# Rewriting the junctures between the branches of an eight-branch transformer kernel: pairs through PSUM, a pinned VectorE order, a shorter root, later transposes

## The chip, the cores and the metric

The program runs on one core of one Trainium2 chip. The metric is the device time of one execution in microseconds (us); of several runs the median counts. The engines are TensorE (PE in the rows, its weight loads PEld), VectorE (DVE), ScalarE (ACT), GpSimd (POOL) and SyncE (SP), which issues the DMAs. SBUF is the working memory, PSUM the memory that TensorE writes to.

## What is computed

Eight branches follow each other on one residual stream x of 512 tokens and 1024 features: two attention blocks, and then twice an FFN, a token mixer and an FFN. Every branch begins with a norm and ends with a norm and an addition:

```python
# attention block            # FFN and mixer of the second part
h = rms_norm(x, pre_norm)    h = swiglu(rms_norm_2(x, g[0]), w_in, w_out)
y = mix(h @ w_in) @ w_out    x = x + 0.5 * rms_norm_2(h, g[1])
x = x + rms_norm(y, post)    h = token_mixer(rms_norm_2(x, g[2]), ...); x = x + rms_norm_2(h, g[3])

def rms_norm(x, g):
    return x * lax.rsqrt(jnp.mean(x * x, axis=-1, keepdims=True) + 1e-6) * g
```

All is float32. Where one branch ends and the next begins lies a juncture: the post norm of y, the addition to x, and the pre norm of the new x. There are seven of them between branches, and the end of the last branch is half of one.

## The kernel before

**Layout.** Activations are transposed: features on the 128 partitions in eight chunks, tokens in the columns, handled in two halves of 256 (`HALF`). `XT` holds x, `Y` (tag `big`) the output of a branch, `xh` and `xl` the normed input of the next branch, split into a high part in a TensorE format (float32r) and the rest. Each product is three matmuls (`mm3`, L238 to L243): high by high, high by low, low by high. Weights are split the same way, high part by ScalarE (L282), rest by GpSimd or VectorE (L283).

**Scales are put off.** The gain is multiplied into xh and xl at once, the reciprocal root of the mean square is not: products are taken of the unscaled x, and their results are multiplied by the row `R` when they leave PSUM. So a norm needs the sum of squares (`square`: ScalarE squares, GpSimd adds, L345), then the sum over partitions by a matmul with ones (`ss_matmul`, L331), the root on VectorE (`rsqrt` and `newton`, L245 to L263: a bit trick and three Newton steps), and two transposes by TensorE that spread it over the partitions (`col_bcast`, L298), copied out of PSUM by ScalarE (L380) into `P` (post norm) or `R` (pre norm).

**The juncture** (`juncture`, L399 to L417) goes, for each half, over eight chunks: VectorE multiplies y by P (L409, or L411 where the gain is still to be multiplied in, which is so behind an FFN), adds it to x (L413), ScalarE makes xh (L372), VectorE xl (L373), ScalarE squares x and GpSimd adds the square. Behind the last branch the sum goes to the output instead, and GpSimd takes eleven of the sixteen additions. P of the first half is made (`post_done`) in the middle of the last products of the old branch.

**The lead** (`lead`, L435 to L468) is the first work of each branch: two weight units of 256 columns by eight chunks, for half 0 with both units chunk by chunk, for half 1 first unit 0 and then unit 1. `pre_cols` (sum and root) and `pre_rows` (transposes and copy) stand between its products, as do the evacuations. A unit and half take two PSUM tiles of 256 columns, one for each 128 output features.

**Order.** The framework's planner orders the instructions of each engine by the order in which they are traced, by when its cost model has their inputs ready, and by `high_priority`, which the root and the copies of its row have. Each engine works through its own queue in order. PSUM has eight banks: four `sc`, two `mm`, two `tp`. Squares and their sums take their buffers from the pool of the lead's weights.

**Names that the prediction uses.** L839 and L115 are VectorE instructions of the attention heads that read one tensor from PSUM and one from SBUF. L1161 are transposes in the mixer's gate chain, whose input is a running sum on VectorE (L1143 to L1146) of the gate product `pg`, evacuated at L1132.

Of the kernel before, what the change touches and what calls it, by code (L numbers as in the profile page):

```python
# [23 lines left out]
F32 = mybir.dt.float32  # L24
# [7 lines left out]
S = 512  # L32
HALF = (slice(0, 256), slice(256, 512))
ALL = slice(0, 512)
D = 1024
# [10 lines left out]
MAGIC = float(0x5F3759DF)  # L46
# [157 lines left out]

class Kern:
    def __init__(self, ctx, tc, ap):
# [4 lines left out]
        self.wp = Pool(ctx.enter_context(tc.tile_pool(name="wp", bufs=3)))  # L211
        self.rp = Pool(ctx.enter_context(tc.tile_pool(name="rp", bufs=2)))
# [5 lines left out]
        self.leads = 0  # L218

# [18 lines left out]
    def mm3(self, out, lhs, rhs, start, stop):  # L238

        nc = self.nc  # L240
        nc.tensor.matmul(out, lhs[0], rhs[0], start=start, stop=False)  # L241
        nc.tensor.matmul(out, lhs[0], rhs[1], start=False, stop=False)  # L242
        nc.tensor.matmul(out, lhs[1], rhs[0], start=False, stop=stop)  # L243

    def rsqrt(self, src, n, mul, add, name, y=None):  # L245

        v = self.nc.vector
        x = self.sm(n, name + "x")
        v.tensor_scalar(x, src, mul, add, op0=OP.mult, op1=OP.add)
        return self.newton(x, n, name, y)  # L250

    def newton(self, x, n, name, y=None):

        v = self.nc.vector
        y = self.sm(n, name + "y") if y is None else y
        t = self.sm(n, name + "t")
        v.tensor_scalar(t.bitcast(I32), x.bitcast(I32), 1, None, op0=OP.logical_shift_right)
        v.tensor_scalar(y.bitcast(I32), t.bitcast(I32), -1.0, MAGIC, op0=OP.mult, op1=OP.add)
        for _ in range(3):
            v.tensor_tensor(t, y, y, op=OP.mult)  # L260
            v.scalar_tensor_tensor(t, t, -0.5, x, op0=OP.mult, op1=OP.mult)
            v.scalar_tensor_tensor(y, t, 1.5, y, op0=OP.add, op1=OP.mult)
        return y  # L263
# [63 lines left out]
    def ss_matmul(self, q, n):  # L327

        p = self.tp()
        for tb in range(n):  # L330
            self.nc.tensor.matmul(p[:, 0, tb:tb + 1], q[:, tb * 128:(tb + 1) * 128], self.ones[:, 0:1],  # L331
                                  start=True, stop=True)
        return p[:, 0, :n]
# [14 lines left out]

    def rms(self, st, y=None):

        x0, x = self.sm(2, "x0"), self.sm(2, "rnx")
        s0 = self.ss_matmul(st["acc"], 2)
        s1 = self.ss_matmul(st["last"], 2) if "last" in st else None
        with self.tc.high_priority():
            if s1 is None:
                return self.rsqrt(s0, 2, 1.0 / D, EPS, "rn", y)
            self.nc.vector.tensor_scalar(x0, s0, 1.0 / D, EPS, op0=OP.mult, op1=OP.add)
            self.nc.vector.scalar_tensor_tensor(x, s1, 1.0 / D, x0, op0=OP.mult, op1=OP.add)
            return self.newton(x, 2, "rn", y)
# [16 lines left out]
    def rows(self, r, out):  # L376

        p = self.col_bcast(r, 2).rearrange("p a b -> p (a b)")
        with self.tc.high_priority():
            self.nc.scalar.copy(out, p[:, 0:256])  # L380

    def pre_cols(self, t):
        self.rms(self.pre[t], self.r[:, 2 * t:2 * t + 2])

    def pre_rows(self, t):
        self.rows(self.r[:, 2 * t:2 * t + 2], self.R[:, HALF[t]])

    def post_done(self, st, t):
        if t == 0:
            self.P = self.lead_pool.tile([128, S], F32, name="P", tag="P", bufs=1)  # L390
        self.rows(self.rms(st), self.P[:, HALF[t]])

    def prenorm(self, g):
        self.next_in()
        for t in range(2):
            for c in range(KC):
                self.pre_chunk(self.pre[t], c, g, HALF[t])

    def juncture(self, Y, gpost, nxt):  # L399


        nc = self.nc
        if nxt:
            self.next_in()
        for t, sl in enumerate(HALF):
            for c in range(KC):
                y, x, P = Y[:, c, sl], self.XT[:, c, sl], self.P[:, sl]
                if gpost is None:
                    nc.vector.tensor_tensor(y, y, P, op=OP.mult)  # L409
                else:  # L410
                    nc.vector.scalar_tensor_tensor(y, y, gpost[:, c:c + 1], P, op0=OP.mult, op1=OP.mult)  # L411
# [23 lines left out]
    def lead(self, evac):  # L435
# [5 lines left out]
        def run(us, t, ks):  # L441
# [1022 lines left out]
```

## Time and profile before

| | us |
|---|---|
| median of three runs | 2952.69 |
| the runs | 2944.2, 2952.69, 2952.72 |
| the profiled execution | 2944.85 |
| its span, first to last instruction | 2942.0 |
| mean granted TensorE clock | 0.977 |

The profile's times are those of one execution, from the start of its span. A row of the timeline merges like instructions that follow each other (x4). "Idle before" is the time that an engine stood still ahead of a group, with what ended it. [...]

### The profile page before, as it was taken

What the parts mean: (1) busy time and instruction counts of PE and PEld (TensorE: products, weight loads), DVE (VectorE), ACT (ScalarE), POOL (GpSimd) and SP (SyncE); (2) the same over time, 40 slices, a digit from 0 to 9 for tenths busy, and PEclk for the clock granted to TensorE, in tenths of its full rate; (3) what the DMA queues carried; (4) which work ended last, traced back from release to release, by engine and by line L of the source; (5) the groups of instructions that cost most, each with busy time, mean ns of one, the idle gap of its engine ahead of it and who ended that gap; (6) DMA issues with size and microseconds to landing.
All of it is one profiled execution on the core that took longest, in us unless ns stands there. A gap on an engine that the chain in (4) does not pass through costs nothing.

```text
span 2942.0 us, 43303 instructions
## 1 busy us (share of the span) xinstructions
PE 2778.2 (94%) x16048; PEld 2427.3 (83%) x16048; DVE 1513.0 (51%) x3398; ACT 1381.3 (47%) x2937; POOL 1347.9 (46%) x1265
## 2 busy tenths in 40 slices
PE   7999999998999988899899998999998899899997
PEld 7997899877888887798888888888887798888886
DVE  6489757987303257857730225312246857731132
ACT  6578547874333334657433334323333648432332
POOL 4553445434444544333444545444453433534545
PEclk9999999999999999999999999999999999999999
DMA  4111211121232212111222322223221220223332
GB/s 170 58 44 51 80 48 44 44 83 62 95 99 97 92 52 80 58 65 60 96 96 88 106 90 69 93 87 108 84 84 48 76 73 30 87 73 94 101 96 74
DMA packets 69283, 230.54 MB, mean 78 GB/s; under 512 B 8968, under 2 KB 11912, under 8 KB 68816
## 3 DMA queue, kind: packets, MB, share of 16 engines
q1 hardware_dynamic: 69072, 227.78, 23.8%
q8 instruction: 126, 2.06, 0.3%
q14 instruction: 85, 0.70, 0.1%
HBM read 225.51 MB, written 2.24 MB: 77 GB/s over the span
## 4 chain that ended last, share of the span: by engine, by line
PE 69%; DVE 20%; ACT 5%; issue 2%; POOL 1%; DMA 1%; DVEq 0%; POOLq 0%; SPq 0%; ACTq 0%
PE sc L242 11%; PE sc L243 11%; PE sc L241 10%; PE mm L241 10%; PE mm L243 10%; PE mm L242 10%; DVE XT L413 2%; DVE xl L373 2%; PE sc L110 1%; PE tp L139 1%; DVE big L411 1%; DVE nm L186 1%; DVE O L1183 1%; DVE E L198 1%; DVE pl L143 1%
## 5 line engine op out<-in xcount | busy, mean ns | idle before, releaser
L283 POOL TENSOR_TENSOR wl<-wr,wh 128x512 fp32r<-128x512 f32 x732 | 943.5, 1299 | 943.1 <-ACT wh L282 905.0
L282 ACT CAST wh<-wr 128x512 fp32r<-128x512 f32 x836 | 502.8, 614 | 733.3 <-PE sc L242 476.7
L242 PE MATMUL sc<-xl,wh 128*128 128x512 f32 (+1 forms) x1600 | 602.9, 377 | 4.3 <-DVE xl L373 4.1
L243 PE MATMUL sc<-xh,wl 128*128 128x512 f32 (+1 forms) x1600 | 601.9, 376 | 0.3 <-DVE wl L283 0.2
L241 PE MATMUL sc<-xh,wh 128*128 128x512 f32 (+1 forms) x1600 | 600.1, 376 | 2.3 <-ACT xh L372 2.2
L484 DVE TENSOR_TENSOR fg<-sc,R 128x512 f32<-128x512 f32 (+1 forms) x88 | 58.7, 667 | 758.8 <-PE sc L243 756.3
L242 PEld LDWEIGHTS sc<-xl,wh 128*128 128x128 f32 x1600 | 307.1, 192 | 59.1 <-DVE xl L373 6.5
L241 PEld LDWEIGHTS sc<-xh,wh 128*128 128x128 f32 x1600 | 305.7, 192 | 55.8 <-ACT xh L372 3.3
L243 PEld LDWEIGHTS sc<-xh,wl 128*128 128x128 f32 x1600 | 307.4, 192 | 53.1 <-DVE wl L283 0.7
L345 POOL TENSOR_TENSOR sacc<-sacc,sq 128x256 f32<-128x256 f32 x222 | 190.3, 864 | 247.3 <-ACT sq L343 223.8
L241 PE MATMUL mm<-wh,xh 128*128 128x256 f32 x1024 | 295.7, 289 | 0.3 <-DVE G L854 0.3
L243 PE MATMUL mm<-wh,xl 128*128 128x256 f32 x1024 | 293.6, 287 | 0.0
L242 PE MATMUL mm<-wl,xh 128*128 128x256 f32 x1024 | 293.5, 287 | 0.0
L243 PE MATMUL mm<-ah,wl 128*128 128x512 f32 (+1 forms) x792 | 289.8, 366 | 0.3 <-POOL wl L283 0.2
L242 PE MATMUL mm<-al,wh 128*128 128x512 f32 (+1 forms) x792 | 289.7, 366 | 0.0
L241 PE MATMUL mm<-ah,wh 128*128 128x512 f32 (+1 forms) x792 | 289.7, 366 | 0.0
L241 PE MATMUL mm<-xh,wh 128*128 128x256 f32 (+1 forms) x784 | 262.6, 338 | 17.2 <-DVE big L667 6.4
L242 PE MATMUL mm<-xl,wh 128*128 128x256 f32 (+1 forms) x784 | 261.2, 333 | 8.2 <-DVE xl L373 8.2
L243 PE MATMUL mm<-xh,wl 128*128 128x256 f32 (+1 forms) x784 | 260.9, 335 | 1.0 <-POOL wl L283 0.9
L241 PEld LDWEIGHTS mm<-wh,xh 128*128 128x128 f32 x1024 | 199.0, 194 | 1.8 <-DVE G L854 0.7
L242 PEld LDWEIGHTS mm<-wl,xh 128*128 128x128 f32 x1024 | 199.1, 194 | 1.5
L243 PEld LDWEIGHTS mm<-wh,xl 128*128 128x128 f32 x1024 | 198.9, 194 | 0.8
(315 smaller groups left out, 5035.6 us busy)
## 6 DMA issues: line engine op xcount, KB each, us to landing
wr<-in_ffn_in_dram SPq DMA_DIRECT2D x176, 512.0 KB, 3.3
wr<-in_ffn_out_dram SPq DMA_DIRECT2D x64, 512.0 KB, 3.5
wr<-in_mix_in_dram SPq DMA_DIRECT2D x56, 512.0 KB, 3.3
wr<-in_w_in_dram SPq DMA_DIRECT2D x48, 512.0 KB, 3.3
wr<-in_ffn_out_dram SPq DMA_DIRECT2D x32, 384.0 KB, 3.1
wr<-in_w_out_dram SPq DMA_DIRECT2D x16, 512.0 KB, 3.3
wr<-in_mix_out_dram SPq DMA_DIRECT2D x16, 512.0 KB, 3.3
Mb<-Md SPq DMA_DIRECT2D x16, 256.0 KB, 3.5
```

The source lines that it names most:

```text
L110: nc.tensor.matmul(sc[:, e], q, kk[:, :n], start=j == 0, stop=j == len(self.K) - 1)
L139: nc.tensor.transpose(p[:, j * per + e], E[i + e][:, j * 128:(j + 1) * 128], self.k.ident)
L143: nc.vector.tensor_tensor(pl[:, :nk, sl], pv, ph[:, :nk, sl].bitcast(F32), op=OP.subtract)
L241: nc.tensor.matmul(out, lhs[0], rhs[0], start=start, stop=False)
L242: nc.tensor.matmul(out, lhs[0], rhs[1], start=False, stop=False)
L243: nc.tensor.matmul(out, lhs[1], rhs[0], start=False, stop=stop)
L282: nc.scalar.copy(hi[:, :m], raw[:, c:c + m])
L283: eng.tensor_tensor(low[:, :m], raw[:, c:c + m], hi[:, :m].bitcast(F32), op=OP.subtract)
L345: nc.gpsimd.tensor_tensor(st["acc"], st["acc"], q, op=OP.add)
L373: nc.vector.scalar_tensor_tensor(lo, x, self.gcol(g, c), hi.bitcast(F32), op0=OP.mult, op1=OP.subtract)
L413: eng.tensor_tensor(x, x, y, op=OP.add)
L484: nc.vector.tensor_tensor(g, ps[0], R[:, sl], op=OP.mult)
```

## The change

A class `Join` replaces `juncture`. The order of its VectorE instructions is fixed with `keep_in_program_order`, which queues an instruction behind the one traced before it on its engine. Work is traced between products by a counter: `after(n, f)` calls f when n further `mm3` have been traced.

- Chunks go in pairs. `front` multiplies two chunks of y by P into a PSUM bank and adds that bank to x with one 512-column instruction; `back` makes the two xl. P is read from PSUM, where the transposes left it; the copy to SBUF is gone. xh stays one chunk at a time, the squares are taken two chunks at once.
- The post norm's sum is traced 4 products into the second half of the old branch's last unit (for a mixer or block: its last two units), its transposes and the first two pairs 8 products later. The second half's sum comes 4 products into the lead, its transposes 9 later.
- The root is a bit trick that is one instruction shorter and two polynomial steps: 9 VectorE instructions in place of 11 (13 where two sums are added). All other roots of the kernel use it too. The sums of both halves of `ss_matmul` now accumulate in PSUM.
- The lead runs both units chunk by chunk in either half, a unit's two results in one PSUM bank. `pre_cols(0)` comes 2 products and `pre_rows(0)` 22 products into the second half; those of the second half go into the products that follow the lead (after 2 and 5, 3 and 7, or 1 and 4 of them). So the tables that need `r` (`rotations`, `tables`) and the gate activations move behind them as well.
- Squares and sums get a pool of their own.

```diff
+class Join:
+    def begin(self, n0, n1):
+        self.k.after(n0, lambda: self.scale(0))
+        self.k.after(n1, self.first)
+    def scale(self, t):
+        self.ry = self.k.rms(self.sts[t])
+    def spread(self, t):
+        self.P[t] = self.k.rows(self.ry, None if t == 0 else self.k.mm().rearrange("p (a b) -> p a b", a=4))
+    def first(self):
+        self.spread(0)
+        if not self.nxt:
+            self.last(0)
+            return
+        self.k.next_in()
+        self.front(0, 0)
+        self.front(0, 1)
+        self.back(0, 0)
+    def finish(self):
...
+        self.back(0, 1)
+        self.front(0, 2)
+        k.after(4, self.second)
+        k.after(9, self.third)
+    def second(self):
+        self.scale(1)
+        self.back(0, 2)
+        self.front(0, 3)
+        self.back(0, 3)
+    def third(self):
+        self.spread(1)
+        self.front(1, 0)
+        self.front(1, 1)
+        self.back(1, 0)
+        self.back(1, 1)
+        self.front(1, 2)
+        self.front(1, 3)
+        self.back(1, 2)
+    def normed(self, t):
+        if t == 0:
+            self.back(1, 3)
+    def front(self, t, i):
...
+        if t not in self.scratch:
+            self.scratch[t] = (k.mm if t else k.sc)().rearrange("p (a n) -> p a n", a=2)
+        s, P = self.scratch[t], self.P[t]
+        if self.gpost is None:
+            put(v.tensor_tensor(s, self.Y[:, c, sl], P[:, None, :].to_broadcast([128, 2, 256]), op=OP.mult))
+        else:
+            for e in range(2):
+                j = 2 * i + e
+                put(v.scalar_tensor_tensor(s[:, e], self.Y[:, j, sl], self.gpost[:, j:j + 1], P, op0=OP.mult, op1=OP.mult))
+        x = k.XT[:, c, sl]
+        put(v.tensor_tensor(x, x, s, op=OP.add))
+        for j in (2 * i, 2 * i + 1):
+            nc.scalar.activation(k.h[0][:, j, sl], k.XT[:, j, sl], AF.Copy, scale=k.gcol(self.nxt[0], j))
+        k.square2(k.pre[t], i, x)
...
+        put(v.tensor_scalar(x, src, mul, add, op0=OP.mult, op1=OP.add))
+        put(v.tensor_scalar(y.bitcast(I32), x.bitcast(I32), -0.5, MAGIC, op0=OP.mult, op1=OP.add))
+        put(v.tensor_tensor(t, y, y, op=OP.mult))
+        put(v.scalar_tensor_tensor(t, t, -RS_B, x, op0=OP.mult, op1=OP.mult))
+        put(v.scalar_tensor_tensor(y, t, RS_A, y, op0=OP.add, op1=OP.mult))
+        put(v.tensor_tensor(t, y, y, op=OP.mult))
+        put(v.tensor_tensor(t, t, x, op=OP.mult))
+        put(v.scalar_tensor_tensor(t, t, RS_C1, t, op0=OP.add, op1=OP.mult))
+        put(v.scalar_tensor_tensor(y, t, RS_C0, y, op0=OP.add, op1=OP.mult))
...
+        run(0)
+        self.after(2, lambda: self.pre_cols(0))
+        self.after(20, lambda: out(0))
+        run(1)
+        self.after(gaps[0], lambda: self.pre_cols(1))
+        self.after(gaps[1], lambda: out(1))
```

## Rows read from the trace of the kernel before

**Rows 1.** Page, part 1: busy us of each engine, share of the span, instructions.

```profile
PE 2778.2 (94%) x16048; PEld 2427.3 (83%) x16048; DVE 1513.0 (51%) x3398; ACT 1381.3 (47%) x2937; POOL 1347.9 (46%) x1265
```

**Rows 2.** Windows: stretch, its us; busy (instructions) PE, PEld, DVE, ACT, POOL; clock, DMA, GB/s.

```profile
340.00:392.00 52.00, 41.11 (x313) 40.25 (x313) 39.41 (x102) 18.46 (x45) 25.16 (x28) 0.93 0.15 48
664.00:712.00 48.00, 37.36 (x283) 36.23 (x282) 39.08 (x96) 20.71 (x49) 23.31 (x26) 0.94 0.16 52
1046.00:1097.00 51.00, 43.50 (x312) 41.24 (x311) 38.50 (x106) 18.90 (x47) 22.96 (x27) 0.90 0.14 44
1406.00:1455.00 49.00, 38.38 (x296) 37.19 (x295) 39.97 (x100) 21.48 (x50) 24.95 (x27) 0.95 0.16 53
1790.00:1837.00 47.00, 39.40 (x264) 37.08 (x263) 37.84 (x97) 20.78 (x49) 22.69 (x22) 0.85 0.14 49
2171.00:2221.00 50.00, 42.49 (x304) 40.54 (x302) 38.81 (x106) 18.63 (x46) 22.19 (x26) 0.90 0.13 40
2532.00:2578.00 46.00, 37.44 (x274) 36.58 (x273) 37.41 (x93) 19.29 (x45) 23.14 (x26) 0.89 0.11 35
2915.00:2942.00 27.00, 11.21 (x87) 10.49 (x86) 17.33 (x50) 2.00 (x5) 10.10 (x12) 0.75 0.23 78
```

**Rows 3.** Timeline of PE, 1046.9 to 1048.2: start us, us, engine, line, operation, shapes.

```profile
1047.08 0.28 PE L243 MATMUL mm<-ah,wl 128*128 128x256 f32 x1
...
1048.04 0.28 PE L242 MATMUL mm<-al,wh 128*128 128x256 f32 x1
```

**Rows 4.** Waits of PE: who waited for whom, us in total, times, longest.

```profile
PE tp L298 <- DVE rny L262: 23.6, 12, 3.0
PE tp L298 <- DVE r L262: 13.1, 6, 3.5
PE tp L1161 <- DVE row L1146: 10.4, 2, 5.2
```

**Rows 5.** Groups by shape, DVE, 1045 to 1097: busy us, mean ns, idle before.

```profile
L411 DVE SCALAR_TENSOR_TENSOR big<-big,ghalf,P 128x256 f32<-128x256 f32 x16 | 10.1, 648 | 1.0 <-ACT P L380 1.0
L373 DVE SCALAR_TENSOR_TENSOR xl<-XT,gains,xh 128x256 fp32r<-128x256 f32 x16 | 9.5, 596 | 0.3 <-ACT xh L372 0.3
L413 DVE TENSOR_TENSOR XT<-XT,big 128x256 f32<-128x256 f32 x16 | 8.6, 547 | 0.0
```

**Rows 6.** Lines L413, L373, L839, L115, whole span: ns min/median/max, first and last start.

```profile
L413 DVE TENSOR_TENSOR XT<-XT,big x117: 407/414/1518, 352.2 to 2938.8; 128x256 f32<-128x256 f32 x117
L373 DVE SCALAR_TENSOR_TENSOR xl<-XT,gains,xh x128: 466/475/1007, 21.8 to 2573.8; 128x256 fp32r<-128x256 f32 x128
L839 DVE TENSOR_TENSOR ra<-mm,lin x24: 399/415/426, 78.1 to 476.7; 128x256 f32<-128x256 f32 x24
L115 DVE CUSTOM_DVE_ANT_0 E<-sc,LC x64: 680/686/693, 1295.5 to 2497.9; 128x512 f32<-128x512 f32 x64
```

**Rows 7.** Timeline of DVE, 1045 to 1060.

```profile
1052.06 0.16 DVE L357 TENSOR_SCALAR x<-tp 128x2 f32<-128x2 f32 x1 [2.44 <-PE tp L331]
...
1054.96 0.16 DVE L262 SCALAR_TENSOR_TENSOR rny<-rnt,rny 128x2 f32<-128x2 f32 x1
1056.11 2.71 DVE L411 SCALAR_TENSOR_TENSOR big<-big,ghalf,P 128x256 f32<-128x256 f32 x2 [0.99 <-ACT P L380]
```

**Rows 8.** Timeline of POOL, 1055 to 1062 and 360 to 370.

```profile
1055.81 5.55 POOL L283 TENSOR_TENSOR wl<-wr,wh 128x512 fp32r<-128x512 f32 x4
...
361.19 7.71 POOL L345 TENSOR_TENSOR sacc<-sacc,sq 128x256 f32<-128x256 f32 x8 [1.97 <-ACT sq L343]
```

**Rows 9.** Timeline of DVE, 362 to 371.

```profile
362.91 0.16 DVE L249 TENSOR_SCALAR rnx<-tp 128x2 f32<-128x2 f32 x1 [0.89 <-PE tp L331]
...
369.73 0.16 DVE L262 SCALAR_TENSOR_TENSOR rny<-rnt,rny 128x2 f32<-128x2 f32 x1
```

**Rows 10.** Timeline of DVE, 2900 to 2942.

```profile
2927.28 0.41 DVE L512 TENSOR_TENSOR big<-mm,big 128x256 f32<-128x256 f32 x1
...
2938.81 0.42 DVE L413 TENSOR_TENSOR XT<-XT,big 128x256 f32<-128x256 f32 x1
```

More of the change, by code (lines that the diff above doesn't have):

```diff
@@ L252, in newton, with mm3 @@
-    def newton(self, x, n, name, y=None):
-        v = self.nc.vector
-        y = self.sm(n, name + "y") if y is None else y
[L256 to L262, printed above, removed]
-        return y
+    def mm3(self, out, lhs, rhs, start, stop, shared=False):
+        mm = self.nc.tensor.matmul
+        mm(out, lhs[0], rhs[0], start=start, stop=False, skip_group_check=shared)
+        mm(out, lhs[0], rhs[1], start=False, stop=False, skip_group_check=shared)
+        mm(out, lhs[1], rhs[0], start=False, stop=stop, skip_group_check=shared)
+        self.tick()
@@ L265, in wload, with after, tick, flush @@
+    def after(self, n, f):
+        self.todo.append([n, f])
+    def tick(self):
+        if self.todo:
+            self.todo[0][0] -= 1
+            if self.todo[0][0] <= 0:
+                self.todo.pop(0)[1]()
+    def flush(self):
+        while self.todo:
+            self.todo.pop(0)[1]()
     def wload(self, src, n=4, lo=None, pool=None, raws=None, cut=False):
@@ L324, in load_x, with ss_matmul @@
             self.nc.sync.dma_start(self.XT[:, k:k + 2], self.ap["xT"][:, k:k + 2])
-    def ss_matmul(self, q, n):
+    def ss_matmul(self, st):
         p = self.tp()
[L330 to L333, printed above, removed]
+        qs = [st["acc"]] + ([st["last"]] if "last" in st else [])
+        for i, q in enumerate(qs):
+            for tb in range(2):
+                self.nc.tensor.matmul(p[:, 0, tb:tb + 1], q[:, tb * 128:(tb + 1) * 128], self.ones[:, 0:1],
+                                      start=i + tb == 0, stop=i == len(qs) - 1, skip_group_check=True)
+        return p[:, 0, :2]
     def square(self, st, c, src, last=False):
@@ L504, in out_unit @@
                                  k == 0, k == FH - 1)
-                        if last and sl.start and b == 0 and k == 6:
-                            self.post_done(sts[0], 0)
                     k = p * 2 + b
@@ L515, in out_unit @@
                             self.square(sts[t], k, Y[0][:, k, h], last=True)
-            if last:
-                self.post_done(sts[1], 1)
+                if last and not sl.start:
+                    self.join = Join(self, Y[0], gpost, sts, nxt)
+                    self.join.begin(4, 8)
         with ExitStack() as es:
@@ L850, in block1, with tables @@
         r, R = self.r, self.R
-        G = self.main.tile([128, KC, S], F32, name="G", tag="big")
+        branch = {}
         def lead_gate(u, sl, ps):
-            for b in range(2):
-                nc.vector.tensor_tensor(G[:, 6 * u + b, sl], ps[b], R[:, sl], op=OP.mult)
-        self.lead(lead_gate)
-        for c in (0, 6):
-            nc.scalar.activation(G[:, c:c + 2], G[:, c:c + 2], AF.Silu)
+            if not branch:
+                branch["G"] = self.main.tile([128, KC, S], F32, name="G", tag="big")
+            nc.vector.tensor_tensor(branch["G"][:, 6 * u:6 * u + 2, sl], ps,
+                                    R[:, None, sl].to_broadcast([128, 2, 256]), op=OP.mult)
+        def tables():
+            for c in (0, 6):
+                nc.scalar.activation(G[:, c:c + 2], G[:, c:c + 2], AF.Silu)
+            rotations()
+        self.lead(lead_gate, (3, 7), tables)
+        G = branch["G"]
         self.lead_es.close()
@@ L1061, in mixer, with ready @@
         r, R = self.r, self.R
-        O = self.main.tile([128, KC, S], F32, name="O", tag="big")
+        branch = {}
         def lead_gate(u, sl, ps):
-            for b in range(2):
-                nc.vector.tensor_tensor(O[:, 4 + 2 * u + b, sl], ps[b], R[:, sl], op=OP.mult)
-        self.lead(lead_gate)
-        nc.scalar.activation(O[:, 4:8], O[:, 4:8], AF.Sigmoid)
+            if not branch:
+                branch["O"] = self.main.tile([128, KC, S], F32, name="O", tag="big")
+            nc.vector.tensor_tensor(branch["O"][:, 4 + 2 * u:6 + 2 * u, sl], ps,
+                                    R[:, None, sl].to_broadcast([128, 2, 256]), op=OP.mult)
+        def ready():
+            nc.scalar.activation(O[:, 4:8], O[:, 4:8], AF.Sigmoid)
+            tables()
+        self.lead(lead_gate, (1, 4), ready)
+        O = branch["O"]
         self.lead_es.close()
```

183 lines of the change are left out of this document (96 added, 87 removed).

## The prediction

> **What bounds the kernel now.** I read the page's first part, then the table of windows, the list of waits, the groups by shape and last the timelines. TensorE is busy for 2778.2 of 2942.0 us [rows 1], so the whole kernel can only give back what TensorE doesn't use. The windows say where that lies. Inside the FFN products nothing is idle; 256-column matmuls start 0.12 us apart at the full clock, eight steps from 1047.08 to 1048.04 [rows 3]. Around each of the seven junctures it is otherwise. In a window that holds only 256-column matmuls and a few shorter ones, the count times 0.12 us is the time that they need: 37.6 of 52 us, 34.0 of 48, 37.4 of 51, 35.5 of 49, 31.7 of 47, 36.5 of 50, 32.9 of 46 [rows 2]. That is 14.4, 14.0, 13.6, 13.5, 15.3, 13.5 and 13.1 us lost, 97.4 us in all and 13.9 on average. The same rows show a granted clock of 0.85 to 0.95: part of the loss is idle time and part is matmuls at the lower of the two clock levels after an idle stretch. Both go together, so I count the sum and not its parts.
>
> The waits name what is late: the transposes of a reciprocal root (`rny` 23.6 us over 12 waits, `r` 13.1 us over 6) [rows 4]; the rest of the juncture waits are products that want `xl` or `xh`. All come from VectorE, which is busy for 37 to 40 us of each window [rows 2]. Its instructions there are slow: over one juncture the 16 multiplies of L411 take 648 ns on average, the 16 adds of L413 547 and the 16 subtractions of L373 596 [rows 5], against medians of 414 (L413) and 475 (L373, and I use it for L411, of the same form) [rows 6]. The slow ones lie beside GpSimd: two multiplies take 2.71 us from 1056.11 [rows 7] while GpSimd works through four weight subtractions from 1055.81 to 1061.36 [rows 8]. Instructions that read PSUM don't show this: L839 never exceeds 426 ns in 24, L115 693 ns at 512 columns in 64, while L413 reaches 1518 [rows 6]. So a juncture is held up by VectorE, and VectorE by GpSimd.
>
> **Multiply and add through PSUM.** The row scale P stays in PSUM and the product y*P goes to a PSUM bank, so each multiply and each add has only one SBUF input. Before: 16 x (0.648 + 0.547 + 0.596) = 28.7 us per juncture. After, behind an FFN: 16 multiplies at 0.475, 8 paired adds at 0.69 (L115's 686 for 512 columns), 16 subtractions still at 0.596, as both of their tensors lie in SBUF: 7.6 + 5.5 + 9.5 = 22.6 us, 6.1 less. Behind a mixer the multiplies are paired too and it is 2.1 us less again. No row shows VectorE writing PSUM. Nearest below is the PSUM read, at the SBUF price (415 against 414); nearest above is the contended price of today (648), by which the multiplies would gain nothing and 2.8 us of the 6.1 would go. A gain over the SBUF price has no reason. I take 415/414, as the operation is the same and only the port's side differs.
>
> A row bears on this: 256 columns cost 415 ns from PSUM (L839) and 414 from SBUF (L413) [rows 6]. [...]
>
> **Shorter root.** A root goes from 12 or 13 instructions to 9, one of them reading PSUM. Undisturbed the 13 take 3.06 us, with one evacuation between (1052.06 to the end of 1054.96) [rows 7]; beside GpSimd 12 take 6.98 (362.91 to the end of 369.73) [rows 9], with other work laid between. At 9/12.5 that is 2.2 to 5.0 us instead of 3.1 to 7.0. With the middle, 5.0 before and 3.6 after, four roots per juncture save 5.6 us. The root is pinned, so nothing comes between; but what is traced behind it waits for it too: the multiplies, adds and subtractions of the next pair, and for those TensorE.
>
> **What leaves the path.** The ScalarE copy of P (0.4 us and two hand-overs) goes, twice a juncture. The `r` transposes of the second half go behind 3 to 10 later products, where 2.2 us per wait (13.1/6) is hidden by them; if that cover were missing, those 2.2 us per juncture come back. In the second half the lead runs both weight units together, so a chunk is used up in 1.44 us (12 x 0.12) and not in 0.72, which doubles the time that VectorE has for it. Squares in pairs leave GpSimd's sums as they are (7 per half).
>
> **A walk through one juncture** (FFN, at about 1049). Today the first multiply starts at 1056.11. The sum placed after 4 triples, the shorter root and no copy make it about 1055.0; the old products end at about 1058.5. Two pairs are through multiply and add by then (2 x 1.64 us), and the first subtractions end at about 1059, with GpSimd's four weight subtractions beside them. From there TensorE wants a pair every 2.9 us and VectorE gives one every 2.8 (2 x 0.475 + 0.69 + 2 x 0.596), with 3.6 us more for each of the two roots in that time. The lead of 3.5 us and the other half's slack cover one of them; I count 0.5 us of stall at the start, 1 at the second sum, 1.5 around the second and third pair, and 1 in the second half: 4 us kept. That regains 9.9 of 13.9 per juncture, below the 11.7 (6.1 + 5.6) that VectorE saves. The bounds: 5 (the lock stays on subtractions and roots) to 12.5 (only the sums' own chain is left). Over seven: 69 us, 35 to 87.
>
> **End, start and side effects.** At the end the last 8 multiplies and 5 VectorE adds run from one P. Today the final evacuation starts at 2927.28, held up by the first half's multiplies, and the last add starts at 2938.81 [rows 10]. After: those multiplies don't contend, so the evacuation comes about 2.5 us sooner, the root is 0.9 shorter, the copy falls away, and the second half's multiplies gain about 1: 4.8 us, between 2 and 6. At the start one wait for `r` goes into later products: 2 us, 0 to 4. Roots inside the heads lose two to three instructions of 0.2 us: 1 us, 0 to 2, as most of them are hidden. On the other side, in the two token mixers the nine table instructions (some 0.16 us each [rows 7]) and the second half's evacuation now lie beside the gate product and may push its evacuation back; the wait behind it (5.2 us each [rows 4]) grows by 1.2 us: minus 2.4, 0 to minus 5. One branch's scales come later, but two banks of evacuation stand between.
>
> **Sum.** 69.4 + 4.8 + 2 + 1 - 2.4 = 74.8 us off the profiled execution of 2944.85: 2870. The median of the runs shown stands 7.8 above that execution, the lowest 0.65 below it; I add 4, about half: 2874.
>
> **Rivals.** *The lock stays (2909).* For: 16 subtractions and 8 of 9 root instructions still have only SBUF operands, and pinned instructions are not overtaken. Such instructions stretch to 1007 and 1518 ns [rows 6]. If the roots take their contended 5.0 us, all 5.6 us saved on them are gone; if the subtractions take 0.8 us, halfway between 0.596 and 1.007, another 3.3 go. Of 11.7 us 2.8 are left, and with the 2.2 us of the `r` wait a juncture gives 5.0: 2944.85 - 35 - 5.4 + 4 = 2909 (5.4 is the sum of the other terms). Against: the first multiplies and adds, the worst today, are free of GpSimd, and they go first. [...]
>
> *Slower: the pinned order (2982).* The roots now stand ahead of multiplies on VectorE, and a root waits for TensorE's sum, which waits for GpSimd's accumulation. GpSimd has had eight of these additions in a row, 7.71 us [rows 8]. Should two roots per juncture wait for such a queue, VectorE and with it TensorE lose 15.4 us where 9.9 were gained, 5.5 each: 2944.85 + 38.5 - 5.4 + 4 = 2982. It decides once a root waits for more than 5 us (9.9/2). Against: today that queue begins only after the old products end, and the additions are spread over a longer time after the change.
>
> *No change (2943).* The new positions set only the traced order. The planner places what isn't pinned by its own costs, and could put sums and transposes on TensorE where it idles again, so that the products wait at other places for as long. Only the other terms would be left: 2944.85 - 5.4 + 4. Against: it is VectorE that is late, and its order is pinned, not planned.
>
> **Chances.** Forecast 0.73, the lock 0.17, no change 0.05, slower 0.05. Below 0.3% (9 us) a measurement of this kernel can't tell a difference, so faster has 0.90, the same 0.05, slower 0.05. The range runs from 2846 (87 us at the junctures and 12 from the better ends of the other terms, on the lowest run) to 2921 (the lock's 35 us, the worse ends of the other terms, 3 us lost, and 8 us for the spread of the runs); outside it are the two small cases and the edges of the large ones.
>
> **What would show it.** Right: juncture windows that lose 3 to 6 us and not 14; multiplies at 475 ns or 415 and paired adds near 690 whatever GpSimd does; roots of about 2 us; no `rny` wait over 1 us; a clock near 1.0. The lock: roots of 5 us and subtractions near 800. The pinned order: long waits of VectorE for TensorE's sums, and of those for GpSimd. A PSUM write priced wrongly: multiplies over 550 ns without GpSimd. I would be wrong mainly if VectorE's pairs come slower than the 2.9 us that TensorE takes for one.

## The result, and the profile after

The changed kernel takes 2870.19 us (median, 2864.3 to 2871.83) beside 2951.64 for the kernel before: a ratio of 0.9726, 95% interval 0.9704 to 0.9747. The forecast was 2874. Its profiled execution took 2871.5 us with a span of 2869.7; that is 73.4 us less than the one of before, where the sum said 74.8. Line numbers in this section are those of the changed kernel: L358 to L360 the three matmuls of a product, L292 the multiply, L294 the paired add, L304 the subtraction that makes `xl`, L369 to L377 the root, L427 the transposes, L412 the weight subtraction, L490 the sum of squares.

The page's busy times, as [rows 1]:

```profile
PE 2752.9 (96%) x16048; PEld 2408.5 (84%) x16048; DVE 1467.5 (51%) x3138; ACT 1365.8 (48%) x2865; POOL 1331.4 (46%) x1265
```

The same matmuls take 25.3 us less of busy time; the mean granted clock of the span is 0.986, and was 0.977. The windows of the seven junctures and of the end, columns as in [rows 2]:

```profile
332.00:380.00 48.00, 46.74 (x379) 45.40 (x378) 34.39 (x90) 16.50 (x36) 29.39 (x44) 1.00 0.16 52
643.00:690.00 47.00, 43.20 (x336) 41.46 (x335) 35.08 (x78) 22.61 (x48) 24.13 (x28) 0.97 0.21 69
1017.00:1062.00 45.00, 40.96 (x324) 40.12 (x323) 33.55 (x73) 16.69 (x35) 22.46 (x30) 0.96 0.15 49
1371.00:1416.00 45.00, 42.12 (x336) 40.45 (x335) 34.71 (x77) 21.69 (x45) 23.32 (x27) 1.00 0.22 71
1741.00:1788.00 47.00, 41.33 (x320) 40.26 (x320) 36.12 (x80) 20.95 (x44) 23.30 (x26) 0.95 0.22 75
2117.00:2162.00 45.00, 40.82 (x324) 40.11 (x324) 33.56 (x73) 16.69 (x35) 22.45 (x30) 0.96 0.15 49
2475.00:2518.00 43.00, 41.21 (x329) 39.65 (x328) 32.03 (x72) 18.66 (x39) 21.25 (x26) 1.00 0.11 37
2844.00:2869.60 25.60, 14.19 (x118) 13.78 (x116) 13.62 (x43) 1.67 (x4) 10.14 (x15) 0.84 0.25 82
```

Counted as in the prediction (PE count times 0.12 us against the length of the window), the seven junctures lose 2.5, 6.7, 6.1, 4.7, 8.6, 6.1 and 3.5 us: 38.2 in place of 97.4. The granted clock stands at 0.95 to 1.00 and not at 0.85 to 0.95. What the lower level cost in the kernel before can be read in its third juncture, columns as in [rows 2], and below them TensorE's timeline (line numbers of that kernel):

```profile
1050.00:1056.00 6.00, 5.93 (x51) 5.76 (x51) 2.43 (x14) 1.35 (x5) 0.88 (x2) 1.00 0.00 1
1062.00:1068.00 6.00, 5.12 (x24) 5.12 (x25) 4.32 (x16) 3.51 (x9) 2.33 (x3) 0.50 0.27 87
```

```profile
1060.82 0.39 PE L241 MATMUL mm<-xh,wh 128*128 128x256 f32 x1 [2.06 <-ACT xh L372]
...
1062.88 0.58 PE L242 MATMUL mm<-xl,wh 128*128 128x256 f32 x1 [1.41 <-DVE xl L373]
...
1063.48 0.41 PE L242 MATMUL sc<-xl,wh 128*128 128x256 f32 x1
1063.69 0.41 PE L243 MATMUL sc<-xh,wl 128*128 128x256 f32 x1
1063.90 0.41 PE L242 MATMUL sc<-xl,wh 128*128 128x256 f32 x1
```

Behind these two waits, at 0.50, 256-column matmuls start 0.21 us apart; at 1.00 it is 0.12 [rows 3].

VectorE in the third juncture, groups by shape from 1017 to 1062, as [rows 5]:

```profile
L304 DVE SCALAR_TENSOR_TENSOR xl<-XT,gains,xh 128x256 fp32r<-128x256 f32 x16 | 10.5, 701 | 0.6 <-ACT xh L296 0.6
L292 DVE SCALAR_TENSOR_TENSOR mm<-big,ghalf,mm 128x256 f32<-128x256 f32 x8 | 3.9, 487 | 0.2
L292 DVE SCALAR_TENSOR_TENSOR sc<-big,ghalf,tp 128x256 f32<-128x256 f32 x8 | 3.9, 487 | 0.3 <-PE tp L427 0.2
L294 DVE TENSOR_TENSOR XT<-XT,sc 128x512 f32<-128x512 f32 x4 | 2.7, 686 | 0.1
L294 DVE TENSOR_TENSOR XT<-XT,mm 128x512 f32<-128x512 f32 x4 | 2.7, 686 | 0.1
```

Multiplies fell from 648 to 487 ns, two adds from 2 x 547 to 686. The subtractions, of the three the only ones that still read two tensors in SBUF, rose from 596 to 701. TensorE's waits, as [rows 4] (us in total, times, longest):

```profile
PE mm L427 <- DVE rny L377: 13.6, 4, 3.6
PE tp L1293 <- DVE row L1278: 9.5, 2, 4.8
PE tp L427 <- DVE r L377: 8.1, 7, 2.0
```

The waits for a root are down from 36.7 us (18 waits) to 21.7 (11). Four are left for the post norm (`rny`), 3.6 us each in the three junctures behind an FFN. What such a root looks like (VectorE's timeline in the third juncture, start us, us):

```profile
1037.06 0.15 DVE L369 TENSOR_SCALAR rnx<-tp 128x2 f32<-128x2 f32 x1
1037.25 0.94 DVE L370 TENSOR_SCALAR rny<-rnx 128x2 int32<-128x2 int32 x1
1038.22 1.18 DVE L371 TENSOR_TENSOR rnt<-rny 128x2 f32<-128x2 f32 x1
1039.43 0.65 DVE L372 SCALAR_TENSOR_TENSOR rnt<-rnt,rnx 128x2 f32<-128x2 f32 x1
1040.11 0.16 DVE L373 SCALAR_TENSOR_TENSOR rny<-rnt,rny 128x2 f32<-128x2 f32 x1
1040.31 0.57 DVE L374 TENSOR_TENSOR rnt<-rny 128x2 f32<-128x2 f32 x1
...
1041.31 0.16 DVE L377 SCALAR_TENSOR_TENSOR rny<-rnt,rny 128x2 f32<-128x2 f32 x1
```

Nothing is laid between, and still four instructions on two elements each take 0.57 to 1.18 us where the others take 0.16. GpSimd's timeline in the same stretch:

```profile
1036.87 2.51 POOL L412 TENSOR_TENSOR wl<-wr,wh 128x512 fp32r<-128x512 f32 x2
1039.33 1.53 POOL L490 TENSOR_TENSOR sacc<-sacc,sq 128x256 f32<-128x256 f32 x2
```

So the forecast's mechanism is there, and so is a part of the rival that the lock (VectorE held up beside GpSimd) stays. Of the forecast's signs, "no `rny` wait over 1 us" failed at these four waits, and four of the seven windows lose more than the 6 us that it allowed. The experiments sort the two, and price the parts one by one.

### The profile page after: what moved, and what is told of

Read it like the earlier page. It is cut to its first block, busy times and chain, and to the rows that moved or that the text cites. A ratio compares the mean times of both kernels' runs of the same rounds, so it can differ in the third digit from the quotient of the medians.

```text
span 2869.7 us, 42890 instructions
## 1 busy us (share of the span) xinstructions
PE 2752.9 (96%) x16048; PEld 2408.5 (84%) x16048; DVE 1467.5 (51%) x3138; ACT 1365.8 (48%) x2865; POOL 1331.4 (46%) x1265
## 4 chain that ended last, share of the span: by engine, by line
PE 72%; DVE 17%; ACT 5%; issue 3%; POOL 2%; DMA 1%; SPq 0%; POOLq 0%; DVEq 0%; ACTq 0%
PE sc L359 11%; PE sc L358 11%; PE sc L360 11%; PE mm L360 10%; PE mm L358 10%; PE mm L359 10%; DVE xl L304 2%; PE sc L116 2%; PE tp L145 2%; DVE O L1315 1%; DVE pl L149 1%; DVE nm L192 1%; PE tp L804 1%; DVE E L204 1%; DVE wl L412 1%
## 5 line engine op out<-in xcount | busy, mean ns | idle before, releaser
L412 POOL TENSOR_TENSOR wl<-wr,wh 128x512 fp32r<-128x512 f32 x732 | 943.5, 1299 | 941.4 <-ACT wh L411 918.1
L411 ACT CAST wh<-wr 128x512 fp32r<-128x512 f32 x836 | 502.6, 612 | 716.4 <-PE sc L359 459.3
L359 PE MATMUL sc<-xl,wh 128*128 128x512 f32 (+1 forms) x1856 | 672.7, 363 | 0.7 <-DVE xl L304 0.6
L358 PE MATMUL sc<-xh,wh 128*128 128x512 f32 (+1 forms) x1856 | 671.3, 363 | 0.0
L360 PE MATMUL sc<-xh,wl 128*128 128x512 f32 (+1 forms) x1856 | 669.8, 361 | 0.0
L359 PEld LDWEIGHTS sc<-xl,wh 128*128 128x128 f32 x1856 | 353.9, 191 | 55.1 <-DVE xl L304 2.8
L360 PEld LDWEIGHTS sc<-xh,wl 128*128 128x128 f32 x1856 | 353.7, 191 | 52.4
L358 PEld LDWEIGHTS sc<-xh,wh 128*128 128x128 f32 x1856 | 352.6, 191 | 52.7
L358 PE MATMUL mm<-wh,xh 128*128 128x256 f32 x1024 | 295.8, 289 | 0.0
L360 PE MATMUL mm<-wh,xl 128*128 128x256 f32 x1024 | 293.8, 287 | 0.0
L360 PE MATMUL mm<-ah,wl 128*128 128x512 f32 (+1 forms) x792 | 289.8, 366 | 0.3 <-POOL wl L412 0.2
L358 PE MATMUL mm<-ah,wh 128*128 128x512 f32 (+1 forms) x792 | 290.0, 366 | 0.0
L358 PEld LDWEIGHTS mm<-wh,xh 128*128 128x128 f32 x1024 | 199.4, 195 | 1.1
L360 PEld LDWEIGHTS mm<-wh,xl 128*128 128x128 f32 x1024 | 199.3, 195 | 1.0
L358 PE MATMUL mm<-xh,wh 128*128 128x512 f32 (+1 forms) x528 | 184.4, 351 | 8.0 <-DVE big L776 3.6
L360 PE MATMUL mm<-xh,wl 128*128 128x512 f32 (+1 forms) x528 | 184.0, 348 | 2.1 <-POOL wl L412 2.1
L359 PE MATMUL mm<-xl,wh 128*128 128x512 f32 (+1 forms) x528 | 182.1, 345 | 0.0
L360 PEld LDWEIGHTS mm<-ah,wl 128*128 128x128 f32 x792 | 149.3, 188 | 25.1 <-POOL wl L412 1.0
```

The lines of the kernel that those rows point to most:

```text
L358: mm(out, lhs[0], rhs[0], start=start, stop=False, skip_group_check=shared)
L359: mm(out, lhs[0], rhs[1], start=False, stop=False, skip_group_check=shared)
L360: mm(out, lhs[1], rhs[0], start=False, stop=stop, skip_group_check=shared)
L411: nc.scalar.copy(hi[:, :m], raw[:, c:c + m])
L412: eng.tensor_tensor(low[:, :m], raw[:, c:c + m], hi[:, :m].bitcast(F32), op=OP.subtract)
```

## The experiments

Times are compared by their ratio to the kernel before on the same chip. The kernel before had medians of 2945.05 us beside the first four kernels, 2948.67 beside the next and 2948.48 beside the last. One thousandth is 2.9 us. The changed kernel, run once more, is the yardstick:

**The changed kernel again (a1_after).**

> The changed kernel once more, as the yardstick of the runs beside it. Both theories: 0.970 to 0.975 of the kernel before, about 2870 us.

Measured 2869.48 us, 0.9731 (0.9717 to 0.9746).

**Back to SBUF (e1_sbuf).** The changed kernel with P and the product in SBUF:

```diff
-        self.P[t] = self.k.rows(self.ry, None if t == 0 else self.k.mm().rearrange("p (a b) -> p a b", a=4))
+        p = self.k.rows(self.ry, None if t == 0 else self.k.mm().rearrange("p (a b) -> p a b", a=4))
+        self.P[t] = self.k.lead_pool.tile([128, 256], F32, name="P", tag="P", bufs=2)
+        with self.k.tc.high_priority():
+            self.nc.scalar.copy(self.P[t], p)
...
-        s, P = self.scratch[t], self.P[t]
+        s, P = self.Y[:, c, sl], self.P[t]
```

> The changed kernel (2870 us), with one part undone: ScalarE copies P to SBUF and the product y*P goes back into y in SBUF; pairs, order, root and lead stay. Theory A (the junctures were held up by VectorE instructions with two SBUF inputs beside GpSimd): the multiplies go from 490 to some 650 ns and the paired adds from 686 to 900 or more, each juncture loses 5 to 8 us again, 2905 to 2925. Theory B (the gain is the order: pinned instructions, places in the products, both units together): the copies and hand-overs alone, mostly hidden, 2870 to 2880.

Measured 2913.73 us, 0.9891 (0.9871 to 0.9912), 0.016 above the yardstick: 47 us lost. Groups by shape of this kernel, VectorE, whole span (L293 and L289 are its multiplies, L295 its paired adds):

```profile
L295 DVE TENSOR_TENSOR XT<-XT,big 128x512 f32<-128x512 f32 x56 | 55.7, 994 | 1.8
L293 DVE SCALAR_TENSOR_TENSOR big<-big,ghalf,P 128x256 f32<-128x256 f32 x48 | 38.5, 842 | 2.4 <-ACT P L234 2.4
L289 DVE TENSOR_TENSOR big<-big,P 128x512 f32<-128x512 f32 x32 | 31.4, 981 | 5.1 <-ACT P L234 5.1
```

994 ns against 686 for the same paired add, where only the place of one operand differs; 842 against 487 for the same multiply, where P and the output have moved. VectorE is busy for 33 us more (1500.3 in place of 1467.5). ScalarE's copies of P are back as well, and their share of the 47 us isn't separated. TensorE now waits for what these instructions feed:

```profile
PE sc L360 <- DVE xl L305: 29.7, 16, 3.1
```

**The long root (e2_longroot).** The changed kernel with the root of before, pinned. With the first instruction, which stays, that is twelve in place of nine, so three more and not the two that the expectation counts (the 11 in the section on the change leave that first one out):

```diff
-MAGIC = float(0x5F1FFFF9)
+MAGIC = float(0x5F3759DF)
...
-        put(v.tensor_scalar(y.bitcast(I32), x.bitcast(I32), -0.5, MAGIC, op0=OP.mult, op1=OP.add))
...
+        put(v.tensor_scalar(t.bitcast(I32), x.bitcast(I32), 1, None, op0=OP.logical_shift_right))
+        put(v.tensor_scalar(y.bitcast(I32), t.bitcast(I32), -1.0, MAGIC, op0=OP.mult, op1=OP.add))
+        for _ in range(3):
+            put(v.tensor_tensor(t, y, y, op=OP.mult))
+            put(v.scalar_tensor_tensor(t, t, -0.5, x, op0=OP.mult, op1=OP.mult))
+            put(v.scalar_tensor_tensor(y, t, 1.5, y, op0=OP.add, op1=OP.mult))
```

> The changed kernel with the old root of 11 instructions, still pinned. Theory A: two instructions of 0.2 us more, up to 1 us each beside GpSimd; the root of the second half stands on the path in the three junctures behind an FFN (TensorE waits 3.6 us for it there already) and at the end: 4 to 15 us slower, 2874 to 2885. Theory B: less than 3 us.

Measured 2884.13 us, 0.9791 (0.9772 to 0.981), 18 us above the yardstick. The waits for the roots grow from 21.7 to 31.6 us.

**Nothing pinned (e3_unpinned).**

```diff
-        self.put = kern.tc.keep_in_program_order
+        self.put = lambda i: i
...
-        put = self.tc.keep_in_program_order if pin else lambda i: i
+        put = lambda i: i
```

> The changed kernel with nothing pinned: the planner orders VectorE in the junctures. Theory A: the pinning matters little, as the instructions are as short as before: 2862 to 2882. Theory B: the planner lays roots, multiplies and subtractions as it did before the change and 25 to 60 us come back, 2895 to 2930.

Measured 2876.75 us, 0.9765 (0.9744 to 0.9787): some 10 us above the yardstick, though the two intervals touch. At most the pinned order helps a little; it is not what the gain rests on.

**Transposes at the lead's end (e4_atlead).** The second half's sum, root, transposes and evacuations are traced right behind the lead:

```diff
-                done()
+                self.after(1, done)
...
-        self.after(gaps[0], lambda: self.pre_cols(1))
-        self.after(gaps[1], lambda: out(1))
+        self.pre_cols(1)
+        out(1)
```

> The changed kernel with the second half's sum, root, transposes and evacuation at the end of the lead instead of 3 to 10 products later. Both theories: TensorE waits at each of eight leads for sum (0.5 us), root (1.9) and row, 2.5 to 3.5 us, and has the lower clock for a stretch after some of them: 20 to 35 us slower, 2890 to 2905. If what comes later hides it anyway: 2870 to 2875.

Measured 2870.89 us, 0.9746 (0.9729 to 0.9763): some 4 us above the yardstick, with intervals that overlap widely, and not the 20 to 35 of the first expectation: its last sentence, that what comes later hides it anyway, came true. TensorE's timeline of this kernel behind the third juncture's lead shows why:

```profile
1064.41 0.50 PE L462 MATMUL tp<-ones,sacc 128*128 128x1 f32 x4
1064.78 0.48 PE L358 MATMUL mm<-xh,wh 128*128 128x512 f32 x1
...
1066.47 0.39 PE L359 MATMUL mm<-xl,wh 128*128 128x512 f32 x1
1066.83 0.40 PE L427 MATMUL tp<-ident,r 128*128 128x128 f32 x2
```

The sum runs at the lead's end, but the planner lays eight matmuls of the next branch ahead of the transposes by itself; over the eight leads it lays 8 to 40. The cover doesn't depend on where the change wrote them.

**One unit after the other (e5_unitwise).**

```diff
-            for k in range(KC):
-                for u in range(2):
+            for k, u in [(k, u) for u in range(2) for k in range(KC)] if t else [(k, u) for k in range(KC) for u in range(2)]:
```

> The changed kernel, but the second half of the lead runs weight unit 0 and then unit 1, so that each chunk is used up in 0.72 us at first and not in 1.44. Theory A (VectorE's supply of chunks is what the lead's second half waits for, and running both units together is what covers it): 10 to 25 us slower, 2880 to 2895. Rival B (the second half's chunks are ready before the lead comes to them): within 4 us of the changed kernel.

Measured 2876.83 us, 0.9754 (0.974 to 0.9769): 7 us above the yardstick, between the two expectations, and the two intervals touch. Using both units per chunk is worth some microseconds at most.

**Only PSUM, on the kernel before (b2_psum).**

```diff
-            self.P = self.lead_pool.tile([128, S], F32, name="P", tag="P", bufs=1)
-        self.rows(self.rms(st), self.P[:, HALF[t]])
+            self.P = []
+        out = None if t == 0 else self.mm().rearrange("p (a b) -> p a b", a=4)
+        self.P.append(self.col_bcast(self.rms(st), 2, out).rearrange("p a b -> p (a b)")[:, 0:256])
...
+            bank = (self.mm if t else self.sc)() if nxt else None
...
+                s = bank[:, c % 2 * 256:c % 2 * 256 + 256] if nxt else y
-                    nc.vector.scalar_tensor_tensor(y, y, gpost[:, c:c + 1], P, op0=OP.mult, op1=OP.mult)
+                    nc.vector.scalar_tensor_tensor(s, y, gpost[:, c:c + 1], P, op0=OP.mult, op1=OP.mult)
-                eng.tensor_tensor(x, x, y, op=OP.add)
+                eng.tensor_tensor(x, x, s, op=OP.add)
...
```

> The kernel before with one edit: the row scale P stays in PSUM and the product y*P goes to a PSUM bank, single chunks, old order, old root (the lead's two units share a bank to make room). Theory A (the lock on multiplies and adds is the largest part of the loss): 30 to 45 us faster than the kernel before, 2907 to 2922. Rival B (it takes the new order and the short root with it): less than 10 us faster, over 2940.

Measured 2880.1 us, 0.9765 (0.9748 to 0.9781). This edit alone gives 68 us, more than either theory allowed, and 87% of what the whole change gives. Its groups by shape, VectorE, whole span (L414 multiplies, L416 adds; the last row writes SBUF, at the kernel's end):

```profile
L416 DVE TENSOR_TENSOR XT<-XT,sc 128x256 f32<-128x256 f32 x56 | 23.1, 413 | 0.6
L414 DVE SCALAR_TENSOR_TENSOR mm<-big,ghalf,mm 128x256 f32<-128x256 f32 x24 | 11.6, 484 | 3.1 <-PE mm L298 2.8
L414 DVE SCALAR_TENSOR_TENSOR big<-big,ghalf,mm 128x256 f32<-128x256 f32 x8 | 3.5, 476 | 0.8 <-PE mm L298 0.8
```

**Its bank sharing alone (c1_banks).** To make room, the two results of a weight unit share a PSUM bank of `sc` in the lead of b2_psum, as they do in the changed kernel. The control has only that:

```diff
-                        new = self.mm if u == t else self.sc
-                        ps[u, t] = [new()[:, 0:256] for _ in range(2)]
+                        bank = self.sc()
+                        ps[u, t] = [bank[:, 0:256], bank[:, 256:512]]
...
```

> The kernel before with the one thing that the kernel with P and product in PSUM (2880) changed beside them: the two weight blocks of a unit share a PSUM bank in the lead. Theory A (the 68 us there come from P and the product alone): within 6 us of the kernel before. Rival B (the freed banks let TensorE or the evacuations go on earlier): 10 us or more faster.

Measured 2939.49 us, 0.9969 (0.9956 to 0.9982): 9 us of the 68, between the two expectations; 60 are left for P and the product. Which wait the freed banks shorten was not found.

**Only the short root, on the kernel before (b1_root).** The eight instructions of the change, with its constants, in place of eleven, unpinned:

```diff
-        v.tensor_scalar(t.bitcast(I32), x.bitcast(I32), 1, None, op0=OP.logical_shift_right)
-        v.tensor_scalar(y.bitcast(I32), t.bitcast(I32), -1.0, MAGIC, op0=OP.mult, op1=OP.add)
-        for _ in range(3):
...
+        v.tensor_scalar(y.bitcast(I32), x.bitcast(I32), -0.5, MAGIC, op0=OP.mult, op1=OP.add)
+        v.tensor_tensor(t, y, y, op=OP.mult)
...
```

> The kernel before with only the root shortened (three instructions less each, old order, P and product in SBUF as before). Theory A (each root is on VectorE's path of the juncture): four roots of some 0.3 us an instruction and seven junctures give 8 to 20 us, so 2929 to 2941 where the kernel before has 2949. Rival B (TensorE waits for the multiplies and adds anyway, so that a shorter root only waits elsewhere): less than 6 us, over 2943.

Measured 2934.26 us, 0.9951 (0.9936 to 0.9966): 14 us.

**PSUM and the short root, old order (b3_psumshort).** b2_psum with b1_root's edit, whose core is again:

```diff
-        v.tensor_scalar(t.bitcast(I32), x.bitcast(I32), 1, None, op0=OP.logical_shift_right)
...
+        v.tensor_scalar(y.bitcast(I32), x.bitcast(I32), -0.5, MAGIC, op0=OP.mult, op1=OP.add)
...
```

> The kernel before with P and product in PSUM and the short root, still in the old order, unpinned, single chunks, transposes at their old places. Theory A (the new order is worth nothing beside these two): 2860 to 2872, as the changed kernel's 2869. Rival B (the order brings what is left): 2874 to 2882, near the 2880 without the short root.

Measured 2879.82 us, 0.9763 (0.9746 to 0.9779): the short root, worth 14 us by itself, adds nothing here. That is rival B's range. VectorE's timeline in the third juncture, at the root that the second half's P waits for:

```profile
1043.90 0.60 DVE L260 TENSOR_SCALAR rny<-rnx 128x2 int32<-128x2 int32 x1
1044.42 1.04 DVE L378 SCALAR_TENSOR_TENSOR xl<-XT,gains,xh 128x256 fp32r<-128x256 f32 x1
1045.39 0.69 DVE L261 TENSOR_TENSOR rnt<-rny 128x2 f32<-128x2 f32 x1
...
1046.39 1.09 DVE L262 SCALAR_TENSOR_TENSOR rnt<-rnt,rnx 128x2 f32<-128x2 f32 x1
1047.40 1.02 DVE L378 SCALAR_TENSOR_TENSOR xl<-XT,gains,xh 128x256 fp32r<-128x256 f32 x1
1048.35 1.24 DVE L263 SCALAR_TENSOR_TENSOR rny<-rnt,rny 128x2 f32<-128x2 f32 x1
...
1051.30 0.36 DVE L267 SCALAR_TENSOR_TENSOR rny<-rnt,rny 128x2 f32<-128x2 f32 x1
```

Eight instructions take 7.8 us (1043.90 to 1051.66): slow ones, with slow subtractions (L378) among them. In b2_psum the same root, of eleven, takes 8.4: here the three that were taken away had cost little. That isn't so everywhere: added up over the 28 roots of the seven junctures, the root's own instructions take 92.5 us in b2_psum and 70.8 here.

**The root in PSUM, on the changed kernel (i1_psumroot).** s, x and t are columns of the sum's PSUM bank; none of ten instructions has two inputs in SBUF:

```diff
+        s, x, t = p[:, 0, 0:2], p[:, 1, 0:2], p[:, 2, 0:2]
...
-            return self.rsqrt(s, 2, 1.0 / D, EPS, "rn", y, pin=True)
+            put(v.tensor_scalar(x, s, 1.0 / D, EPS, op0=OP.mult, op1=OP.add))
+            put(v.tensor_scalar(y.bitcast(I32), x.bitcast(I32), -0.5, MAGIC, op0=OP.mult, op1=OP.add))
+            put(v.tensor_tensor(t, y, x, op=OP.mult))
+            put(v.scalar_tensor_tensor(t, t, -RS_B, y, op0=OP.mult, op1=OP.mult))
...
```

> The changed kernel with the norm's root (sum over the partitions) in ten instructions whose x and t lie in PSUM, so that none of them has two SBUF inputs. Theory A (what is left of the roots' time, 4.4 us for one beside GpSimd against 1.7 us undisturbed, is the lock between VectorE and GpSimd): the root behind an FFN takes 1.7 to 2.2 us, the waits for it fall from 3.6 us each to about 1, and the time falls by 5 to 12 us to 2858 to 2865. Rival B (it is long because of what is laid between its instructions, or because VectorE waits for the next PSUM access each time): the root stays at 4 us or more and the time is 2868 to 2876.

Measured 2856.1 us, 0.9687 (0.9673 to 0.9702): 13 us below the changed kernel. The same root as above, VectorE's timeline of this kernel:

```profile
1035.72 0.16 DVE L499 TENSOR_SCALAR tp<-tp 128x2 f32<-128x2 f32 x1
1035.91 0.16 DVE L500 TENSOR_SCALAR rny<-tp 128x2 int32<-128x2 int32 x1
1036.10 0.17 DVE L501 TENSOR_TENSOR tp<-rny,tp 128x2 f32<-128x2 f32 x1
...
1037.50 0.16 DVE L508 SCALAR_TENSOR_TENSOR rny<-rny,tp 128x2 f32<-128x2 f32 x1
1037.57 1.63 DVE L304 SCALAR_TENSOR_TENSOR xl<-XT,gains,xh 128x256 fp32r<-128x256 f32 x2
```

1.9 us, beside the same two weight subtractions on GpSimd. Over the whole span the slowest of 32 instructions of one of its lines is as quick as the quickest (ns min/median/max):

```profile
L502 DVE SCALAR_TENSOR_TENSOR tp<-tp,r x16: 168/168/169, 56.5 to 2507.6; 128x2 f32<-128x2 f32 x16
L502 DVE SCALAR_TENSOR_TENSOR tp<-tp,rny x16: 168/168/169, 340.7 to 2847.9; 128x2 f32<-128x2 f32 x16
```

and TensorE's waits for roots are 8.8 us in place of 21.7:

```profile
PE tp L427 <- DVE r L508: 5.5, 5, 2.2
PE mm L427 <- DVE rny L508: 3.3, 4, 2.0
```

Whether it is GpSimd that stretches these instructions can be counted in the traces, by asking of each one whether it overlaps in time with a two-tensor instruction of GpSimd. Of the instructions of the 28 roots in the junctures of the kernel before, 251 overlap with none, and none of them exceeds 171 ns; of the 91 that do, 65 take more than 250 ns, up to 1275. The adds of L413 are alike: 425 ns at most in the 53 that overlap with none, up to 1518 in the other 64. In i1_psumroot 110 root instructions overlap with GpSimd's, and none exceeds 169 ns.

**The same in the old order (b4_psumroot).** b3_psumshort with that root:

```diff
+        x, t = s0[:, 1, 0:2], s0[:, 2, 0:2]
+        y, u = self.sm(2, "rny") if y is None else y, self.sm(2, "rnt")
...
+            v.tensor_tensor(t, y, x, op=OP.mult)
+            v.scalar_tensor_tensor(t, t, -RS_B, y, op0=OP.mult, op1=OP.mult)
...
```

> The same with the root's x and t in PSUM, so that no instruction of the root has two SBUF inputs; old order still. Theory A (lock and root length are all that matters): 2850 to 2862, as the changed kernel with such a root (2856). Rival B (the new order is needed): 10 us or more above that kernel, 2866 to 2880.

Measured 2855.88 us, 0.9685 (0.967 to 0.9699). That is i1_psumroot's time without the new order, the pins, the pairs and the moved transposes. It beats both kernels, and is the smaller edit of the kernel before.

## Why the prediction came out right

**What bounds the kernel: right.** VectorE held up the junctures and GpSimd held up VectorE. e1_sbuf shows it by the place of P and the product (994 against 686 ns, 47 us), i1_psumroot by the root (4.4 against 1.9 us, 13 us), and the count of overlaps names GpSimd (root instructions of up to 1275 ns where they overlap with its own, of 171 at most where they don't).

**The price of a PSUM write: right.** The bounds were 415/414 of the SBUF price and the contended 648. A multiply that writes PSUM takes 484 ns and one that writes SBUF 476 (b2_psum), so the step is 8 ns.

**Multiply and add: the term was too small.** 6.1 us per juncture make 43 us over seven. b2_psum against c1_banks gives 60, though VectorE's multiplies and adds lose only 33 us of busy time in it (138.7 before, summed over L409, L411 and L413; 105.3 after). The rest wasn't split by an experiment. ScalarE's copy of P and its hand-overs left too, and TensorE is busy for 16.9 us less with the same matmuls (2772.6 in c1_banks, 2755.7 in b2_psum), at a mean granted clock of 0.986 and not 0.978. Taking only 9.9 of 11.7 us per juncture from VectorE to TensorE was a wrong discount for this part.

**Root: the term was too large, and not additive.** 5.6 us per juncture make 39. The short root gives 14 us alone, 0 beside PSUM in the old order, 18 in the new one. "9/12.5 of the time", which is 0.72, held for VectorE: the own instructions of the 28 roots in the junctures take 94.5 us before and 69.1 with the short root alone (0.73), 92.5 and 70.8 beside PSUM (0.77), 78.0 in e2_longroot and 58.5 in the changed kernel (0.75). The step that failed is the one from VectorE's time to TensorE's: 25.4 us saved there gave 14, 21.7 gave nothing, 19.5 gave 18 (the kernel's other roots were shortened in these runs too). Beside PSUM in the old order TensorE's waits for the roots even grew, from 22.2 us (b2_psum) to 25.0 (b3_psumshort); why is open. This error and that of the multiplies and adds partly cancel in 69.4, which is why the sum looks better than its terms.

**What is kept per juncture: 5.5 us, not 4.** 38.2 us over seven, so 59.2 were regained and not 69.4. The prediction named both causes as the lock's rival and gave it 0.17 (its sum makes 2908, not 2909): subtractions near 800 ns (701) and roots of 5 us (4.4, in three junctures of seven). The lock did stay, on a part. As a whole the rival is refuted: it needed all roots at 5 us, and twelve of the post norm's sixteen took 1.7.

**The transposes' cover: a misread wait.** 2.2 us per juncture were to come back without it, taken from the six waits for `r` of the kernel before. None of the six is the second half's. They all stand ahead of the first half's transposes, one of them at the kernel's start; the second half's already had 24 to 44 matmuls between sum and transposes, and waited for nothing. TensorE's timeline of the kernel before, the two halves behind the first juncture:

```profile
385.05 0.41 PE L298 MATMUL tp<-ident,r 128*128 128x128 f32 x2 [3.49 <-DVE r L262]
393.38 0.40 PE L298 MATMUL tp<-ident,r 128*128 128x128 f32 x2
```

So there was nothing to gain at the second half's, and e4_atlead, where the planner keeps a cover besides, lost some 4 us in all, within the intervals of the two runs. What did shrink are the first half's waits, from 13.1 to 7.5 of the 8.1 us that are left: 60 to 73 matmuls now stand between sum and transposes there, in place of 18 to 37.

**End, start, mixers.** The end, from the start of the last product to the end of the span, shrinks from 17.9 us (2924.08 to 2942.0) to 13.2 (2856.53 to 2869.7): 4.7, where 4.8 was forecast. At the start the first evacuation of v (ScalarE) begins at 83.2 and not at 89.9 us: 6.7, where 2 was forecast, with 0 to 4 as bounds. Of this 2.3 us are the wait for `r` that the forecast meant; for the same 553 matmuls up to there TensorE is also busy for 3.0 us less (74.3 and 71.3, at a granted clock of 0.94 and 0.96) and stands still for 1.4 us less elsewhere, which the forecast had left out. The mixers were to cost 2.4 us; their gate chain's wait is 9.5 us and not 10.4 [rows 4], so they cost nothing there. 59.2 + 4.7 + 6.7 = 70.6 of the 72.3 us between the spans. That 73.4 us came so near the 74.8 of the sum is partly luck: the junctures gave 10.2 less than forecast, and the start 4.7 more and the mixers' unpaid 2.4 made up for most of it.

**The other rivals.** The pinned order didn't turn against TensorE: without it (e3_unpinned) the kernel is not faster, but some 10 us slower. "No change, as the planner re-places what isn't pinned" is refuted by the result, but half its idea is right: b4_psumroot reaches the best time with the planner's own order.

**What the parts are worth in sum.** By the ratios: bank sharing 9 us, P and product in PSUM 60, the short root beside them 0, the new order with pairs and pins 9 (b3_psumshort to a1_after, whose intervals touch); the root in PSUM would add 13 to the change, or 23 to the old order, and then the new order is worth nothing (0.9685 against 0.9687).

## What to carry to other kernels

When small VectorE instructions stretch in places, look at what GpSimd does in the same microseconds before touching the order or the count of instructions: keeping the row scale and the product in PSUM gave 60 us here, taking a quarter of a root's instructions away between 0 and 18. Price a shorter chain by what the engine that waits for it gets back, not by what it saves on its own engine, and look up which of two like waits is the long one before pricing its cover. And test each part of such a change alone on the old kernel, since gains needn't add (the short root gave 14 us alone and 0 beside PSUM), and two wrong terms can make a right sum.

## What the hardware showed beyond that

Instructions whose one input tensor lies in SBUF were held up too: L370 (`tensor_scalar`, integers) took 0.94 us above. Four of the sixteen that write `rny` overlap with a two-tensor instruction of GpSimd and take 615 to 949 ns; the other twelve take 170 at most. Of the 33 of L369 that read PSUM, 13 overlap, and none exceeds 160. The instructions of L370 over the whole span of the changed kernel, and those of L369, of the same operation, whose input lies in PSUM for `rnx` and in SBUF for the `rdx` shown:

```profile
L370 DVE TENSOR_SCALAR rny<-rnx x16: 168/169/949, 338.4 to 2858.7; 128x2 int32<-128x2 int32 x16
L370 DVE TENSOR_SCALAR rdy<-rdx x14: 158/172/1208, 169.6 to 2331.9; 128x4 int32<-128x4 int32 x8, 128x8 int32<-128x8 int32 x6
```

```profile
L369 DVE TENSOR_SCALAR rnx<-tp x33: 145/158/160, 22.9 to 2858.5; 128x2 f32<-128x2 f32 x33
L369 DVE TENSOR_SCALAR rdx<-df x6: 157/272/1276, 169.3 to 573.5; 128x8 f32<-128x8 f32 x6
```

So L369 took 160 ns at most from PSUM (128x2) and up to 1276 from SBUF (128x8).
